# Score products of two lower halves side by side on TensorE's rows, and both stick-breaking heads chunk by chunk

## The chip, the cores and the metric

The kernel runs on one core of a Trainium2 chip. The metric is the device time of one execution in microseconds (us); the number that counts is the median of several executions of the same program. The engines are TensorE (PE; PEld is its weight load), VectorE (DVE), ScalarE (ACT), GpSimd (POOL) and SyncE (SP), which issues all DMAs here.

## The reference

One layer of a streaming encoder, for a prompt of 2048 frames and for 8 running streams of 16 new frames with 512 cached ones. The input is normed and modulated, projected to queries, keys, values and gates, and goes through two branches side by side: differential attention (A, 4 heads with two components of 64 each) and stick-breaking attention (B, 8 heads of 64). Outputs are gated, merged and projected.

```python
def diff_attention(q, k, v, qpos, kpos, lam):
    s = jnp.einsum('bqhcd,bkhcd->bhcqk', q, k) * (HEAD_DIM_A ** -0.5)
    mask = (kpos // CHUNK)[None, :] <= (qpos // CHUNK)[:, None]
    p = jax.nn.softmax(jnp.where(mask, s, -jnp.inf), axis=-1)
    w = p[:, :, 0] - lam * p[:, :, 1]
    return jnp.einsum('bhqk,bkhe->bqhe', w, v)

def stick_breaking_attention(q, k, v, qpos, kpos):
    z = jnp.einsum('bqhd,bkhd->bhqk', q, k) * (HEAD_DIM_B ** -0.5)
    mask = kpos[None, :] < qpos[:, None]
    log_1m = jnp.where(mask, jax.nn.log_sigmoid(-z), 0.0)
    log_a = jax.nn.log_sigmoid(z) + lax.cumsum(log_1m, axis=3, reverse=True) - log_1m
    a = jnp.where(mask, jnp.exp(log_a), 0.0)
    return jnp.einsum('bhqk,bkhd->bqhd', a, v)
```

## The kernel before

Everything runs in float16 pairs: a float32 number is cut into an upper half `hi` (float16 of the scaled number) and a lower half `lo` (float16 of the rest), and a product is hi·hi + hi·lo + lo·hi, added up in PSUM.

The work is cut into eight units (`units`, u = 0 to 7). Even units are of kind 0 (A: one head with its two components c), odd units of kind 1 (B: two heads, also called c). Each unit goes over 17 tiles of 128 rows: first the sample tile (t = 16, `NT`: the 16 new frames of all 8 streams), then the prompt's tiles t = 0 to 15. One pair (u, t) is a step. Per step:

- `project` multiplies the tile's hidden states (`hg`, fetched from `hT_d`) with the unit's weights (L409), and in `gate_piece` a share of the gate columns (L476). Its `finish` cuts query, key and value into halves. For a component c the key is kept as [hi; lo] (64 + 64 columns), the query as [hi; hi] and as [lo; 0], the zeros being written once.
- `transpose_qk` turns these with TensorE: two transposes for k (L489), four for q (L493), into one bank of PSUM, then copies them to `k` and `qst` in SBUF (L503, L504; ACT for A, DVE for B).
- `scores` forms, for every chunk `ch` of 512 keys up to the diagonal and for each c, one piece: the product [hi; hi]·[hi; lo] (L611), the product [lo; 0]·[hi; lo] (L612), and on the diagonal a mask, multiplied by an identity (L615). Each piece takes one PSUM bank of tag "s", of which there are three.
- `evacuate` reads the bank. For A, DVE scales it into `sc_p` or `sc_n` and takes the maximum (L530); after the diagonal chunk `softmax_pair` follows. For B, ACT writes the sigmoid of the score to `sc_p` and the sigmoid of its negative back to the bank (both L121), and `stick` runs a scan on DVE from the bank to `sc_n` (L588), from the last key to the first. When a segment of up to 8 blocks (`SEG`) is through, `stick_weights` multiplies on POOL (L594), and `turn` cuts the weights into halves (L544, L545) and transposes them by a DMA on SP's queue (L552) into `wt`.
- `pv` multiplies the weights with the values two steps later (`PV_LAG`): L659 to L661 for A, L663 and L664 for B.

The pieces of a step are laid side by side by `interleave`, which places each stream's pieces evenly by their costs; a score piece of a full chunk has cost 2.0. The projection runs ahead of the scores by a lead. In A the order of score pieces is chunk by chunk with both components; in B it is all chunks of the first head from the diagonal back, then all of the second:

```python
order = [(c, ch) for ch in range(nch) for c in range(2)] if kind == 0 else \
        [(c, ch) for c in range(2) for ch in reversed(range(nch))]
```

A scheduler orders each engine's instructions at compile time from this code, by dependences and free buffers, so the order on PE isn't always that of the code. Buffers that matter: `BANKS = {"mm": 2, "s": 3, "t": 1, "o": 2}` in PSUM, `SC_BUFS = 6` each for `sc_p` and `sc_n`, `WT_BUFS = 5`.

After the last unit comes the output stage: per tile the branches (L1227) and the output projection (L1266), and beside them, in `sample`, the sample tile's attention over cached keys. There `keys` cuts cached keys (POOL L271, DVE L274) and transposes them by DMA, `queries` spreads the sample queries into `qpad` (L705), and `scores_all` multiplies them with the new keys (L727 to L729) and the cached keys (L735, four matmuls on 32 columns of the array each).

Of the kernel before, what the change touches and what calls it, by code (L numbers as in the profile page):

```python
# [25 lines left out]
P = 128  # L26
# [4 lines left out]
NS = 16  # L31
# [80 lines left out]
def layer_kernel(ctx: ExitStack, tc: tile.TileContext, a: dict):  # L112
# [54 lines left out]
    g_d = [dram.tile([P, 2 * D], F32, name=f"g_d{t}") for t in range(NT + 1)]  # L167
    s_d = [dram.tile([P, 8, P], F16, name=f"s_d{u}") for u in range(8)]
    gate_d = dram.tile([9, D], F32, name="gate_d")
# [208 lines left out]
    qs = c01.enter_context(tc.tile_pool(name="qs", bufs=1))  # L378
    qbuf = [qs.tile([P, 2, 2, 2, 64], F16, name=f"qbuf{i}") for i in range(2)]
    for qb in qbuf:  # L380
        G.memset(qb[:, 1, :, 1, :], 0.0)
    at_hand, ahead = {}, {}
# [5 lines left out]
    def project(U, t):  # L388
# [30 lines left out]
        def finish():  # L419
# [9 lines left out]
            def halves(dst, src, scale):  # L429
                src = src.rearrange("p (c d) -> p c d", d=64)  # L430
                split(dst[:, :, 0, :], dst[:, :, 1, :], src, scale, S)

            def query(src, scale):
                src = src.rearrange("p (c d) -> p c d", d=64)
                S.activation(out=qb[:, 0, :, :, :], in_=src.unsqueeze(2).to_broadcast([P, 2, 2, 64]), func=AF.Identity, scale=scale)
                V.scalar_tensor_tensor(out=qb[:, 1, :, 0, :], in0=src, scalar=scale, in1=qb[:, 0, :, 0, :], op0=ALU.mult, op1=ALU.subtract)
            if kind == 0:
                cosT, sinT = box["r"][:, 0:32], box["r"][:, 32:96]
                x4 = pr[:, 0:256].rearrange("p (c f d) -> p c f d", c=4, f=2)
                rot = stg.tile([P, 256], F32, tag="rot", name="rot")  # L440
                r2 = stg.tile([P, 256], F32, tag="r2", name="r2", bufs=1)
                G.tensor_tensor(out=rot.rearrange("p (c f d) -> p c f d", c=4, f=2), in0=x4,  # L442
                                in1=cosT.unsqueeze(1).unsqueeze(1).to_broadcast([P, 4, 2, 32]), op=ALU.mult)
# [4 lines left out]
                halves(vt, p[:, 256:384], s2)  # L448
                query(rot[:, 0:128], s)
                halves(k16, rot[:, 128:256], s)  # L450
            else:
                rot = pr
                halves(vt, p[:, 256:384], s2)
                halves(k16, p[:, 128:256], s2)
                query(p[:, 0:128], s2)
# [6 lines left out]
            if t == NT:  # L462
                load(out=s_d[U["u"]][:, 6:8, :], in_=vt.rearrange("p c f d -> p c (f d)"))
            U["q16", t], U["k16", t] = qb, k16
# [19 lines left out]
    def transpose_qk(U, t):  # L484
        g, i = t // 4, t % 4
        q16, k16 = U.pop(("q16", t)), U.pop(("k16", t))
        pt = bank("t", F16)
        for c in range(2):
            T.transpose(pt[:, c * P : (c + 1) * P], k16[:, c, :, :].rearrange("p f d -> p (f d)"), id16)  # L489
        for f in range(2):  # L490
            for c in range(2):
                j = 2 + f * 2 + c
                T.transpose(pt[:, j * P : (j + 1) * P], q16[:, f, c, :, :].rearrange("p r d -> p (r d)"), id16)  # L493
        if t == NT:
            sam = stg.tile([P, 6, P], F16, tag="sam", name="sam", bufs=1)
            qst, kst = sam[:, 0:4, :], sam[:, 4:6, :]
        else:
            if i == 0:
                U["k"][g] = kvp.tile([P, 2, 512], F16, tag="k", name="k", bufs=K_BUFS)
            U["q", t] = qst = stg.tile([P, 4, P], F16, tag="qst", name="qst", bufs=Q_BUFS)  # L500
            kst = U["k"][g][:, :, i * P : (i + 1) * P]
        copy = V.tensor_copy if U["kind"] == 1 else S.copy
        copy(out=kst, in_=pt[:, 0:256].rearrange("p (c n) -> p c n", c=2))  # L503
        copy(out=qst, in_=pt[:, 256:768].rearrange("p (j n) -> p j n", j=4))  # L504
        if t == NT:
            load(out=s_d[U["u"]][:, 0:6, :], in_=sam)

# [89 lines left out]
    def scores(U, t, jobs):  # L597
# [5 lines left out]

        def chunk(c, ch):
            job = own[c if kind == 1 else 0]
            seg = job["segs"][ch * 4 // SEG]
# [4 lines left out]
            T.matmul(p[:, 0:n], qst[:, c, :], kk[:, c, 0:n], start=True, stop=False)  # L611
            T.matmul(p[:, 0:n], qst[:, 2 + c, :], kk[:, c, 0:n], start=False, stop=not diag)  # L612
            if diag:
                m = mask_a if kind == 0 else mask_b
                T.matmul(p[:, n - m.shape[1] : n], idb, m, start=False, stop=True)  # L615
            evacuate(job, seg, c, p, ch * 512 - seg["lo"] * P, n, sc[:, 3:4], sc[:, 4:5], ch)
            if kind == 0:
                if diag and c == 1:
                    softmax_pair(job)
                return  # L620
            i = job["segs"].index(seg)
            later = job["segs"][i + 1] if i + 1 < len(job["segs"]) else None
            stick(seg, later, ch * 512 - seg["lo"] * P, n, p)
            if ch * 4 == seg["lo"]:
                if later is not None:
                    stick_weights(job, later, None)
                if i == 0:
                    stick_weights(job, seg, later)
# [56 lines left out]
    def sample(U, dec, qpad, cs):  # L685
# [8 lines left out]
        def fetch():  # L694

            box["s"] = sam = dec.tile([P, 8, P], F16, tag="dsam", name="dsam", bufs=2)
            load(out=sam, in_=s_d[U["u"]])
# [5 lines left out]
        def queries():  # L703
            for r in range(2):
                V.tensor_copy(out=qpad.rearrange("p j (i r) n -> p j i r n", r=2)[:, :, :, r, r * NS : (r + 1) * NS],  # L705
                              in_=box["s"][:, 0:4, :].rearrange("p j (i r s) -> p j i r s", r=2, s=NS)[:, :, :, r, :])

# [4 lines left out]
        def keys(i):  # L712
            kc = box.pop((nk, i))
            k16 = dec.tile([P, 16, 2, 64], F16, tag="k16c", name="k16c", bufs=2)
            split(k16[:, :, 0, :], k16[:, :, 1, :], kc.rearrange("p j (c d) -> p (j c) d", c=2), sk, G)
            box["k", i] = kt = dec.tile([P, 8, 2, P], F16, tag="dks", name="dks", bufs=4)
            nc.sync.dma_start_transpose(out=kt.rearrange("p j c n -> p (j c) n"), in_=k16.rearrange("p j f d -> p (j f d)"))

        def scores_all():

            box["jobs"] = [new_job(U, t, c, 5, dec) for c in range(heads)]
            qsam, kn = box["s"][:, 0:4, :], box["s"][:, 4:6, :]
            mask = mask_as if kind == 0 else mask_bs
            pn = bank("s")
            for c in range(2):
                p = pn[:, c * P : (c + 1) * P]
                T.matmul(p, qsam[:, c, :], kn[:, c, 0:P], start=True, stop=False)  # L727
                T.matmul(p, qsam[:, 2 + c, :], kn[:, c, 0:P], start=False, stop=False)
                T.matmul(p, idb, mask, start=False, stop=True)  # L729
            for c in range(2):  # L730
# [7 lines left out]
                seg = job["segs"][0]  # L738
                evacuate(job, seg, c, pn[:, c * P : (c + 1) * P], 512, P, sc[:, 3:4], sc[:, 4:5], 1)
                evacuate(job, seg, c, pc, 0, 512, box["f"][:, 0:1], box["f"][:, 1:2], 0)  # L740
                if kind == 1:
                    stick(seg, None, 512, P, pn[:, c * P : (c + 1) * P])
                    stick(seg, None, 0, 512, pc)
                    stick_weights(job, seg, None)
# [26 lines left out]
        def finish():  # L771
            po = bank("s")
            vn = box["s"][:, 6:8, :].rearrange("p c (f d) -> p c f d", f=2)
            for job in box["jobs"]:
# [565 lines left out]
```

## Time and profile before

| | |
|---|---|
| median of 3 runs | 2507.16 us (2504.18 to 2513.22) |
| the profiled execution | 2508.37 us, span 2506.5 us |
| mean granted TensorE clock | 0.94 |
| instructions in the trace | 45283 |

The span runs from the first to the last instruction of the profiled execution; its own time is 1.9 us longer than its span. In the profile, L612 is line 612 of the kernel, `out<-in` are the program's tile names, and "idle before" is the time for which the engine stood still ahead of an instruction, with what released it. A matmul's duration is its passage through the array, and passages overlap. By the instructions that read the score banks, A units' scores are worked on from about 160 to 304, 581 to 775, 1019 to 1223 and 1469 to 1679 us, those of B units from about 335 to 575, 783 to 1013, 1231 to 1463 and 1691 to 1905 us, and the output stage from about 1910 us.

### The profile page before, as it was taken

The numbers are of one execution on the slowest core, as the hardware profiler recorded it, in microseconds if no ns is written. First come the engines' busy times: TensorE is split into PE (matmuls) and PEld (weight loads), VectorE is DVE, ScalarE is ACT, GpSimd is POOL, SyncE is SP. The second block draws the span as 40 slices with busy tenths as digits, with TensorE's granted clock in tenths as the row PEclk, the third lists the DMA queues.
The fourth block names the chain that finished last, engine by engine and source line by source line (L and its number), as shares of the span: only waits on it lengthen the run. The fifth ranks groups of instructions, "written<-read, shape, count | busy, mean of one in ns | idle before, by whom it ended". The sixth has DMA issues, their size and how long they took to land. (4 is left out here: it accounts for less than half of the span.)

```text
span 2506.5 us, 45283 instructions
## 1 busy us (share of the span) xinstructions
PE 2195.5 (88%) x16366; PEld 1275.3 (51%) x16366; DVE 1793.3 (72%) x3762; ACT 1602.7 (64%) x3200; POOL 827.6 (33%) x671
## 2 busy tenths in 40 slices
PE   7859898899999988889989888999975788889997
PEld 3435555455655555556655555555543344444443
DVE  3577846877676678757577876656787888888765
ACT  2558757787767688657678876656775545445542
POOL 1543113354211244311034442102344454544422
PEclk8979999999999999999999999999985799899999
DMA  9578878998787899767679976656678989888531
GB/s 287 183 221 206 211 175 200 196 220 191 180 193 185 198 222 212 172 152 183 157 192 194 219 190 177 160 132 142 153 168 206 257 224 242 242 212 229 167 111 51
DMA packets 890994, 477.07 MB, mean 190 GB/s; under 512 B 540074, under 2 KB 842330, under 8 KB 890256
## 3 DMA queue, kind: packets, MB, share of 16 engines
q1 hardware_dynamic: 890768, 474.17, 76.6%
q8 instruction: 128, 2.10, 0.4%
q14 instruction: 98, 0.80, 0.1%
HBM read 272.94 MB, written 73.44 MB: 138 GB/s over the span
## 5 line engine op out<-in xcount | busy, mean ns | idle before, releaser
L409 PE MATMUL ps_mm<-wpair,hg 128*128 128x512 f16 x3120 | 789.7, 388 | 58.1 <-DMA hg<-hT_d 54.4
L594 POOL TENSOR_TENSOR sc_p<-sc_p,sc_n 128x127 f32<-128x127 f32 (+7 forms) x192 | 314.0, 1639 | 807.3 <-DVE sc_n L588 796.0
L409 PEld LDWEIGHTS <-hg 128*128 128x128 f16 x3120 | 281.9, 100 | 328.9 <-DMA hg<-hT_d 62.5
L476 PE MATMUL ps_t<-gw,hg 128*128 128x256 f16 (+1 forms) x2856 | 397.6, 293 | 2.3 <-DVE qst L504 2.3
L476 PEld LDWEIGHTS <-hg 128*128 128x128 f16 x2856 | 280.4, 100 | 96.0 <-DVE qst L504 2.6
L588 DVE TENSOR_TENSOR_SCAN sc_n<-ps_s,sc_n,zero_t 128x512 f32<-128x512 f32 x192 | 245.6, 1279 | 63.4 <-ACT ps_s L121 58.2
L611 PE MATMUL ps_s<-k,qst 128*128 128x512 f16 (+3 forms) x640 | 226.5, 355 | 53.3 <-DVE sc_n L588 41.2
L545 DVE TENSOR_TENSOR sc_n<-sc_p,sc_n 128x128 f16<-128x128 f32 (+7 forms) x192 | 229.7, 1201 | 39.2 <-ACT sc_n L544 38.8
L121 ACT ACTIVATE sc_p<-ps_s,usc 128x512 f32<-128x512 f32 (+3 forms) x320 | 205.0, 641 | 47.1 <-PE ps_s L612 25.6
L612 PE MATMUL ps_s<-k,qst 128*128 128x512 f16 (+3 forms) x640 | 226.3, 356 | 0.0
L1227 PE MATMUL ps_mm<-wb,uT 128*128 128x512 f16 x816 | 206.8, 407 | 20.5 <-DVE o L1125 12.5
L121 ACT ACTIVATE ps_s<-ps_s,usc 128x512 f32<-128x512 f32 (+3 forms) x328 | 199.9, 610 | 0.0
L1266 PE MATMUL ps_o<-wo,yT 128*128 128x512 f16 x816 | 193.0, 390 | 6.9 <-ACT wo L269 2.4
L663 PE MATMUL ps_o<-v,wt 128*128 128x128 f16 x1088 | 156.5, 226 | 39.8 <-DMA wt<-sc_n 39.7
L544 ACT CAST sc_n<-sc_p 128x128 f16<-128x128 f32 (+7 forms) x192 | 154.8, 813 | 49.5 <-POOL sc_p L594 48.7
L442 POOL TENSOR_TENSOR rot<-pr,rope 128x256 f32<-128x256 f32 x68 | 59.8, 879 | 351.8 <-ACT pr L423 293.7
L251 ACT ACTIVATE junk<-wst 128x1024 f16<-128x1024 f32 x124 | 131.6, 1062 | 47.2 <-DMA wst<-in_w_in_dram 17.4
L663 PEld LDWEIGHTS <-wt 128*128 128x128 f16 x1088 | 104.0, 102 | 90.3 <-DMA wt<-sc_n 49.7
L1227 PEld LDWEIGHTS <-uT 128*128 128x128 f16 x816 | 82.7, 104 | 125.3 <-issue 50.8
L530 DVE TENSOR_SCALAR_CACHE_REDUCE sc_n<-ps_s,usc 128x512 f32<-128x512 f32 (+3 forms) x160 | 106.6, 666 | 55.2 <-PE ps_s L615 34.2
L664 PE MATMUL ps_o<-v,wt 128*128 128x64 f16 x1088 | 145.2, 198 | 0.0
L530 DVE TENSOR_SCALAR_CACHE_REDUCE sc_p<-ps_s,usc 128x512 f32<-128x512 f32 (+3 forms) x160 | 106.5, 666 | 52.6 <-PE ps_s L612 41.7
(295 smaller groups left out, 4372.9 us busy)
## 6 DMA issues: line engine op xcount, KB each, us to landing
hg<-hT_d SPq DMA_DIRECT2D x130, 512.0 KB, 4.5
wst<-in_w_in_dram SPq DMA_DIRECT2D x112, 256.0 KB, 3.8
g<-g_d SPq DMA_DIRECT2D x34, 512.0 KB, 5.8
wst<-in_w_in_dram SPq DMA_DIRECT2D x32, 512.0 KB, 4.8
out_dram<-pr SPq DMA_DIRECT2D x204, 64.0 KB, 2.3
g_d<-gt SPq DMA_DIRECT2D x102, 128.0 KB, 3.1
wide<-in_w_ada_dram SPq DMA_DIRECT2D x12, 1024.0 KB, 10.3
z_d<-pr SPq DMA_DIRECT2D x136, 64.0 KB, 1.8
```

The costliest lines, as they stand in the source:

```text
L121: i = S.activation(**kw)
L409: T.matmul(box["p"], box["h"][:, hi, k, :], U["w"][k][:, wi, :], start=(n == 0), stop=(n == 3 * KT - 1))
L476: T.matmul(box["g"][:, 0:gw], box["h"][:, hi, k, :], U["wg"][k // per][:, k % per, wi, :], start=(j == 0), stop=(j == 3 * KT - 1))
L530: V.tensor_scalar(out=dst[:, lo : lo + n], in0=p[:, 0:n], scalar1=sc_pos, scalar2=None, op0=ALU.mult, op1=ALU.max, accum_out=job["mx"][:, ...
L545: V.tensor_tensor(out=lo, in0=src, in1=hi, op=ALU.subtract)
L588: V.tensor_tensor_scan(out=dst[:, lo : lo + n][:, ::-1], data0=src[:, 0:n][:, ::-1], data1=zero_t[:, 0:1].to_broadcast([P, n]), initial=fi ...
L594: G.tensor_tensor(out=p[:, 0:m], in0=p[:, 0:m], in1=n[:, 1 : m + 1], op=ALU.mult)
L611: T.matmul(p[:, 0:n], qst[:, c, :], kk[:, c, 0:n], start=True, stop=False)
L612: T.matmul(p[:, 0:n], qst[:, 2 + c, :], kk[:, c, 0:n], start=False, stop=not diag)
L663: T.matmul(po[:, c * P : (c + 1) * P], wt[:, wj, :], vt[:, c, :, :], start=first, stop=False)
L1227: T.matmul(pb, st["u"][:, ui * 8 + br * 4 + k, :], wb[:, br, wi, k, c], start=(n == 0), stop=(n == 11))
L1266: T.matmul(po, st["y"][:, yi * 8 + k, :], wo[:, wi, k, c], start=(n == 0), stop=(n == 3 * KT - 1))
```

## The change

For both components together, the query is now kept as [hi; hi] of the first, [hi; hi] of the second, and one tile [lo of the first; lo of the second]. The second component's key is stored as [lo; hi], so that the upper 64 rows of the array meet lo·hi of the first component and the lower 64 rows lo·hi of the second. The new function `multiply` does a chunk for both components: two full products (with the mask behind each on the diagonal), each into a bank of its own, then two products of 64 rows, one on each half of the array's rows. One transpose per tile, the zeros in `qbuf` and one of the eight parts of `s_d` go.

A score piece is now a chunk with both components or heads, with twice the cost, and takes two "s" banks. For B this means that both heads are worked on chunk by chunk in turn, from the diagonal back, and that the scans and weights of both come behind the pair of products. In `sample`, `keys` cuts the two components in separate instructions with the halves in the order above, `queries` copies in eight small instructions for two, and `scores_all` uses one bank "s" and one bank "t" for the new keys, with 64-row products last.

```diff
-            k16 = stg.tile([P, 2, 2, 64], F16, tag="k16", name="k16")
+            k16 = stg.tile([P, 4, 64], F16, tag="k16", name="k16")
...
+            def keys(src, scale):
+                split(k16[:, 0::3, :], k16[:, 1:3, :], src.rearrange("p (c d) -> p c d", d=64), scale, S)
...
-                S.activation(out=qb[:, 0, :, :, :], in_=src.unsqueeze(2).to_broadcast([P, 2, 2, 64]), func=AF.Identity, scale=scale)
-                V.scalar_tensor_tensor(out=qb[:, 1, :, 0, :], in0=src, scalar=scale, in1=qb[:, 0, :, 0, :], op0=ALU.mult, op1=ALU.subtract)
+                S.activation(out=qb[:, 0:4, :].rearrange("p (c r) d -> p c r d", r=2), in_=src.unsqueeze(2).to_broadcast([P, 2, 2, 64]), func=AF.Identity, scale=scale)
+                V.scalar_tensor_tensor(out=qb[:, 4:6, :], in0=src, scalar=scale, in1=qb[:, 0:4:2, :], op0=ALU.mult, op1=ALU.subtract)
...
-        copy(out=qst, in_=pt[:, 256:768].rearrange("p (j n) -> p j n", j=4))
+        copy(out=qst, in_=pt[:, 256:640].rearrange("p (j n) -> p j n", j=3))
...
+    def multiply(pc, q, k, mask):
+        for c in range(2):
+            T.matmul(pc[c], q[:, c, :], k[:, c, :], start=True, stop=False)
+            if mask is not None:
+                n = pc[c].shape[1]
+                T.matmul(pc[c][:, n - mask.shape[1] : n], idb, mask, start=False, stop=False)
+        for c in range(2):
+            r = slice(c * 64, c * 64 + 64)
+            T.matmul(pc[c], q[r, 2, :], k[r, c, :], start=False, stop=True)
...
-            p = bank("s")
+            pc = [bank("s") for _ in range(2)]
...
-            T.matmul(p[:, 0:n], qst[:, c, :], kk[:, c, 0:n], start=True, stop=False)
-            T.matmul(p[:, 0:n], qst[:, 2 + c, :], kk[:, c, 0:n], start=False, stop=not diag)
...
+            multiply([p[:, 0:n] for p in pc], qst, kk[:, :, 0:n], None if not diag else mask_a if kind == 0 else mask_b)
+            for c, p in enumerate(pc):
+                job = own[c if kind == 1 else 0]
+                seg = job["segs"][ch * 4 // SEG]
+                evacuate(job, seg, c, p, ch * 512 - seg["lo"] * P, n, sc[:, 3:4], sc[:, 4:5], ch)
...
+            for c, p in enumerate(pc):
...
+                stick(seg, later, ch * 512 - seg["lo"] * P, n, p)
...
-        order = [(c, ch) for ch in range(nch) for c in range(2)] if kind == 0 else \
-                [(c, ch) for c in range(2) for ch in reversed(range(nch))]
-        return [(2.0 if ch < t // 4 else (t % 4 + 1) / 2, lambda c=c, ch=ch: chunk(c, ch)) for c, ch in order]
+        return [(4.0 if ch < t // 4 else t % 4 + 1, lambda ch=ch: chunk(ch)) for ch in (range(nch) if kind == 0 else reversed(range(nch)))]
...
+            def copy(dst, src, rows):
+                for r in range(2):
+                    V.tensor_copy(out=qpad[rows, dst, :, :].rearrange("p (i r) n -> p i r n", r=2)[:, :, r, r * NS : (r + 1) * NS],
+                                  in_=box["s"][rows, src, :].rearrange("p (i r s) -> p i r s", r=2, s=NS)[:, :, r, :])
+            for c in range(2):
+                copy(c, c, slice(0, P))
+                copy(2 + c, 2, slice(c * 64, c * 64 + 64))
...
-            k16 = dec.tile([P, 16, 2, 64], F16, tag="k16c", name="k16c", bufs=2)
-            split(k16[:, :, 0, :], k16[:, :, 1, :], kc.rearrange("p j (c d) -> p (j c) d", c=2), sk, G)
+            k16 = dec.tile([P, 8, 2, 2, 64], F16, tag="k16c", name="k16c", bufs=2)
+            for c in range(2):
+                split(k16[:, :, c, c, :], k16[:, :, c, 1 - c, :], kc[:, :, c * 64 : c * 64 + 64], sk, G)
...
-            pn = bank("s")
+            pn = [bank(tag)[:, 0:P] for tag in "st"]
```

More of the change, by code (lines that the diff above doesn't have):

```diff
@@ L167, in layer_kernel @@
     g_d = [dram.tile([P, 2 * D], F32, name=f"g_d{t}") for t in range(NT + 1)]
-    s_d = [dram.tile([P, 8, P], F16, name=f"s_d{u}") for u in range(8)]
+    s_d = [dram.tile([P, 7, P], F16, name=f"s_d{u}") for u in range(8)]
     gate_d = dram.tile([9, D], F32, name="gate_d")
@@ L378, in layer_kernel @@
     qs = c01.enter_context(tc.tile_pool(name="qs", bufs=1))
-    qbuf = [qs.tile([P, 2, 2, 2, 64], F16, name=f"qbuf{i}") for i in range(2)]
-    for qb in qbuf:
-        G.memset(qb[:, 1, :, 1, :], 0.0)
+    qbuf = [qs.tile([P, 6, 64], F16, name=f"qbuf{i}") for i in range(2)]
     at_hand, ahead = {}, {}
@@ L447, in finish @@
                 G.tensor_tensor(out=rot, in0=rot, in1=r2, op=ALU.add)
-                halves(vt, p[:, 256:384], s2)
+                values(p[:, 256:384], s2)
                 query(rot[:, 0:128], s)
-                halves(k16, rot[:, 128:256], s)
+                keys(rot[:, 128:256], s)
             else:
                 rot = pr
-                halves(vt, p[:, 256:384], s2)
-                halves(k16, p[:, 128:256], s2)
+                values(p[:, 256:384], s2)
+                keys(p[:, 128:256], s2)
                 query(p[:, 0:128], s2)
@@ L462, in finish @@
             if t == NT:
-                load(out=s_d[U["u"]][:, 6:8, :], in_=vt.rearrange("p c f d -> p c (f d)"))
+                load(out=s_d[U["u"]][:, 5:7, :], in_=vt.rearrange("p c f d -> p c (f d)"))
             U["q16", t], U["k16", t] = qb, k16
@@ L487, in transpose_qk @@
         pt = bank("t", F16)
[L488 to L493, printed above, removed]
+        for x16, n, lo in ((k16, 2, 0), (q16, 3, 2)):
+            for c in range(n):
+                T.transpose(pt[:, (lo + c) * P : (lo + c + 1) * P], x16[:, 2 * c : 2 * c + 2, :].rearrange("p f d -> p (f d)"), id16)
         if t == NT:
-            sam = stg.tile([P, 6, P], F16, tag="sam", name="sam", bufs=1)
-            qst, kst = sam[:, 0:4, :], sam[:, 4:6, :]
+            sam = stg.tile([P, 5, P], F16, tag="sam", name="sam", bufs=1)
+            qst, kst = sam[:, 0:3, :], sam[:, 3:5, :]
         else:
@@ L499, in transpose_qk @@
                 U["k"][g] = kvp.tile([P, 2, 512], F16, tag="k", name="k", bufs=K_BUFS)
[L500 removed]
+            U["q", t] = qst = stg.tile([P, 3, P], F16, tag="qst", name="qst", bufs=Q_BUFS)
             kst = U["k"][g][:, :, i * P : (i + 1) * P]
@@ L602, in scores, with chunk @@
         jobs += own
-        def chunk(c, ch):
-            job = own[c if kind == 1 else 0]
-            seg = job["segs"][ch * 4 // SEG]
+        def chunk(ch):
             n = 512 if ch < t // 4 else (t % 4 + 1) * P
-            p = bank("s")
+            pc = [bank("s") for _ in range(2)]
             qst, kk = U["q", t], U["k"][ch]
             diag = ch == t // 4
[L611 to L616, printed above, removed]
+            multiply([p[:, 0:n] for p in pc], qst, kk[:, :, 0:n], None if not diag else mask_a if kind == 0 else mask_b)
[3 more added lines that the diff above has]
+                evacuate(job, seg, c, p, ch * 512 - seg["lo"] * P, n, sc[:, 3:4], sc[:, 4:5], ch)
@@ L617, in chunk @@
             if kind == 0:
-                if diag and c == 1:
+                if diag:
                     softmax_pair(job)
                 return
[L621 to L628, printed above, removed]
@@ L630, in scores @@
-        order = [(c, ch) for ch in range(nch) for c in range(2)] if kind == 0 else \
-                [(c, ch) for c in range(2) for ch in reversed(range(nch))]
-        return [(2.0 if ch < t // 4 else (t % 4 + 1) / 2, lambda c=c, ch=ch: chunk(c, ch)) for c, ch in order]
+            for c, p in enumerate(pc):
+                job = own[c]
+                seg = job["segs"][ch * 4 // SEG]
+                i = job["segs"].index(seg)
+                later = job["segs"][i + 1] if i + 1 < len(job["segs"]) else None
+                stick(seg, later, ch * 512 - seg["lo"] * P, n, p)
+                if ch * 4 == seg["lo"]:
+                    if later is not None:
+                        stick_weights(job, later, None)
+                    if i == 0:
+                        stick_weights(job, seg, later)
@@ L694, in fetch @@
         def fetch():
-            box["s"] = sam = dec.tile([P, 8, P], F16, tag="dsam", name="dsam", bufs=2)
+            box["s"] = sam = dec.tile([P, 7, P], F16, tag="dsam", name="dsam", bufs=2)
             load(out=sam, in_=s_d[U["u"]])
```

27 lines of the change are left out of this document (11 added, 16 removed).

## The prediction

> **What bounds the kernel now.** I read the page first: busy shares and costliest groups. The chain that ended last (second row) covers 4% of the span, at its end, so it says nothing about the scores. For those I used busy time by stretch, then PE's waits.
>
> ```profile
> PE 2195.5 (88%) x16366; PEld 1275.3 (51%) x16366; DVE 1793.3 (72%) x3762; ACT 1602.7 (64%) x3200; POOL 827.6 (33%) x671
> ...
> PE 2%; DVE 1%; DMA 1%; ACT 0%; issue 0%; POOL 0%; DVEq 0%; POOLq 0%; ACTq 0%
> ```
>
> ```profile
> core 0: us, PE busy (x) PEld busy (x) DVE busy (x) ACT busy (x) POOL busy (x), PEclk, DMA share, GB/s
> ...
> 1010.00:1240.00 230.00, 215.64 (x1670) 138.25 (x1669) 151.85 (x393) 149.88 (x336) 41.12 (x46) 0.97 0.69 167
> 1240.00:1450.00 210.00, 184.83 (x1441) 115.29 (x1439) 160.86 (x247) 158.94 (x317) 82.74 (x59) 0.94 0.89 197
> ...
> 1690.00:1910.00 220.00, 192.64 (x1367) 104.50 (x1365) 173.03 (x257) 154.37 (x294) 85.96 (x53) 0.92 0.69 154
> 1910.00:2506.00 596.00, 500.80 (x3740) 253.16 (x3740) 458.74 (x973) 279.04 (x450) 250.66 (x179) 0.90 0.73 197
> ```
>
> The first stretch is an A unit (PE 94% busy), the next two are B units (88%, with DVE and ACT at 70 to 79%), the last is the stage of cached keys and outputs. PE sets the pace of A. In B, PE still has the most work, but it is held up:
>
> ```profile
> engine line waited for: us in total, times, longest us
> PE ps_mm L409 <- DMA hg<-hT_d: 54.4, 29, 5.7
> PE ps_s L611 <- DVE sc_n L588: 41.2, 39, 3.1
> PE ps_o L663 <- DMA wt<-sc_n: 39.7, 32, 6.5
> PE ps_o L659 <- DMA wt<-sc_n: 22.4, 19, 3.7
> ...
> PE ps_s L611 <- DVE sc_n L530: 3.4, 4, 1.5
> ```
>
> The second row is a score matmul waiting for a bank of PSUM: there are three "s" banks, and a B bank comes back when the scan (L588) has read it. For A (L530 reads the bank) the same wait is 3.4 us. So removed PE time counts nearly in full in A, and a new wait on banks would appear first in B.
>
> **The score matmuls: what is removed.** One score piece now is two full matmuls, L611 and L612. Their forms:
>
> ```profile
> L612 PE MATMUL ps_s<-k,qst 128*128 128x512 f16 x448 | 174.4, 389 | 0.0
> ...
> L612 PE MATMUL ps_s<-k,qst 128*128 128x384 f16 x64 | 21.4, 335 | 0.0
> ...
> L612 PE MATMUL ps_s<-k,qst 128*128 128x256 f16 x64 | 17.7, 277 | 0.0
> ...
> L612 PE MATMUL ps_s<-k,qst 128*128 128x128 f16 x64 | 14.1, 222 | 0.0
> ```
>
> The 389 ns are a matmul's passage, not its price; the price is the distance between starts.
>
> ```profile
> start us, us, engine line op out<-in xcount [idle before <-releaser]
> 82.54 0.59 PE L409 MATMUL ps_mm<-wpair,hp 128*128 128x512 f16 x2
> 83.06 0.41 PE L923 MATMUL ps_t<-ident,tmp 9*128 9x9 f32 x4
> ...
> 1563.01 0.39 PE L493 MATMUL ps_t<-id,qbuf 128*128 128x128 f16 x4
> ...
> 2192.66 0.59 PE L1266 MATMUL ps_o<-wo,yT 128*128 128x512 f16 x2
> 2193.19 1.91 PE L735 MATMUL ps_s<-dks,qpad 128*32 128x512 f16 x32
> 2195.03 0.39 PE L1227 MATMUL ps_mm<-wb,uT 128*128 128x512 f16 x1
> ```
>
> Two matmuls of 512 columns take 0.59 us, one 0.38, so starts lie 0.21 to 0.22 us apart; I use 0.216. Four of 128 columns take 0.39 and one 0.22: 0.056 apart. The price follows the columns: 0.162 for 384, 0.108 for 256.
>
> A row's count is of both components, so there are 224 pairs of 512 columns and 32 of each shorter form, 320 in all. Of four full matmuls per pair the change leaves two, plus two half-height ones. If the halves run together, a pair loses one matmul: 224 x 0.216 + 32 x (0.162 + 0.108 + 0.056) = 48.4 + 10.4 = 58.8 us.
>
> Do they run together? No 64-row pair is in this trace. The nearest row is L735, where four matmuls use 32 columns of the array each: 32 of 512 columns in 1.91 us, where one after the other they would need 32 x 0.216 = 6.9. Separate strips of the array therefore do overlap, almost perfectly. Bounds for the pair: one matmul (full overlap) to two (none, 58.8 us lost again). I take full overlap, as L735 shows for strips the other way round.
>
> **What is added: changing the shape of the array.** The second L1266 starts at 2192.66 + 0.59 - 0.38 = 2192.87, and L735, of another shape, at 2193.19: about 0.31 us later, not 0.216. On the way out the last group of L735 starts at 2193.19 + 1.91 - 0.39 = 2194.71 and L1227 at 2195.03: again about 0.31. The 9-row transposes L923 show it for rows: the second L409 starts at 82.75, L923 at 83.06. So each change costs about 0.095 us more than a matmul of the same shape. That is about the 100 ns of one weight load, which between matmuls of one shape lies under the matmul before:
>
> ```profile
> L612 PEld LDWEIGHTS <-qst 128*128 128x128 f16 x640 | 63.1, 99 | 87.8 <-issue 56.1
> ```
>
> Every pair goes in and out: 320 x 2 x 0.095 = 60.8 us. Against 58.8 us saved this is +2 us: pairs of 512 columns gain 0.026 us, those of 384, 256 and 128 lose 0.03, 0.08 and 0.13. Bounds: nothing, if the two halves count as no other shape, to a full emptying of the array, 0.38 - 0.216 + 0.10 = 0.26 us a change, 166 us in all. The three rows agree on 0.095 and I take that.
> The Trainium skill, page "TensorEngine Tiling (Array Packing)", section "Key Properties", says that changing the tiling mode drains TensorE. Read as a full drain it gives the 166 us just named and 105 us more in the sum; the rows here show less, since L735 begins before the last L1266 has ended.
>
> **Transposes and their copies.** Six transposes a tile become five: 136 tiles x 0.056 = -7.6 us on PE (L493 counts 544, four a tile). The copy of q's transposes shrinks from 512 to 384 elements:
>
> ```profile
> L504 ACT COPY qst<-ps_t 128x512 f16<-128x512 f16 x64 | 38.0, 593 | 0.0
> ...
> L504 DVE COPY qst<-ps_t 128x512 f16<-128x512 f16 x64 | 26.5, 414 | 0.0
> ...
> L503 ACT COPY k<-ps_t 128x256 f16<-128x256 f16 x64 | 23.4, 365 | 11.7 <-PE ps_t L493 11.5
> ```
>
> By the 593 and 365 ns of 512 and 256 elements ACT saves some 0.11 us in each of 68 tiles, 7.8 us, and DVE rather less. Both engines have 20% and more idle time, so I count nothing. Splitting q and k keeps its sizes.
>
> **Two banks at a time.** This is where I expect the loss. Up to now a piece takes one of three banks, and the bank is wanted again three pieces later. A B unit has 80 pieces in its 210 to 230 us, 2.75 us each, so a bank has 8.2 us. After the change a pair takes two banks together: the second product of the next pair needs the first bank of this pair, two piece-times, or 5.5 us, later. How long a bank is held:
>
> ```profile
> 1835.03 0.38 PE L611 MATMUL ps_s<-k,qst 128*128 128x512 f16 x1
> ...
> 1836.33 0.68 ACT L121 ACTIVATE sc_p<-ps_s,usc 128x512 f32<-128x512 f32 x1
> ...
> 1836.91 0.65 ACT L121 ACTIVATE ps_s<-ps_s,usc 128x512 f32<-128x512 f32 x1
> ...
> 1837.66 1.27 DVE L588 TENSOR_TENSOR_SCAN sc_n<-ps_s,sc_n,zero_t 128x512 f32<-128x512 f32 x1
> ```
>
> From 1835.03 to 1838.93, 3.9 us. In a pair, ACT can start on the first head only when the lower halves are through, 0.216 + 0.31 + 0.39 = 0.92 us after the first product; two sigmoids (1.33) and a scan (1.27) return that bank after 3.5 us with no queue, and the second, behind the first on ACT, after 4.9. With queues as in the rows, a us more each. The margin falls from 8.2 - 3.9 = 4.3 us to 5.5 - 4.5 = 1 us, and pieces are not evenly spaced. PE works in order: behind the waiting product stand that pair's lower halves, the next projection and the weighted values, and ACT and DVE wait for these in turn.
>
> Bounds for what is added: nothing, if the order of PE's work is laid so that other matmuls fill the gap, up to each of the 160 B pairs waiting the 1.06 us of a present wait (41.2 / 39), 170 us. Nearest is the present wait itself: I let it double, +41 us. Some of that covers time that PE would have waited for hg or wt anyway (116.5 us in three rows), so I count 60%, +25 us. A is left out: two reads of 0.75 us each by L530 return its banks, and it hardly waits today.
>
> Both heads' weights now come together at the end of a tile, and the "n" buffers of both (six in all, four of them for a tile above 8 blocks) are held at once. The values use them two tiles later, so this delays transposing DMAs on SP's queue, behind which hg loads stand, but should not end the tile; zero, with the risk in the upper end.
>
> **The last stage.** Cached keys are cut in two instructions in place of one on POOL and on DVE:
>
> ```profile
> L271 POOL TENSOR_SCALAR k16c<-dc,s_c 128x1024 f16<-128x1024 f32 x32 | 41.7, 1302 | 78.5 <-DMA dc<-in_cache_a_k_dram 27.3 <-DMA dc<-in_cache_b_k_dram 23.5 <-issue 13.6
> ...
> L271 POOL TENSOR_SCALAR wpair<-wst,sw 128x512 f16<-128x512 f32 x28 | 23.8, 857 | 69.7 <-DMA wst<-in_w_in_dram 47.4 <-PE ps_mm L409 9.6 <-PE ps_s L615 8.4
> ...
> L705 DVE COPY qpad<-dsam x16: 195/220/1211, 1938.2 to 2304.7; 128x256 f16<-128x256 f16 x16
> ```
>
> POOL: 64 x 0.857 - 41.7 = +13 us, under cover, as POOL is 42% busy there. DVE has 77% in that stage and gains small copies: 64 for 16 at 0.2 us each at most, +10 us. The new scores of a unit change shape four times, 8 x 4 x 0.095 = 3 us on PE. I take +5 us for the stage, between 0 and 15.
>
> **Sum**, against the profiled execution (2508.4 us, span 2506.5; 1.2 us above the median): +2 - 7.6 + 25 + 5 = +24, so 2532 us, and 2531 on the median.
>
> **The rivals.** First, on the other side: changing to half rows costs nothing, because weights of one half are loaded under the matmul before. Then the 58.8 and 7.6 us come off: with the bank waits and the last stage as above 2507 - 66 + 30 = 2471, without them 2441. Against it stand L923 and L735, where the change shows every time; for it, that neither is a 64-row half. It decides if the change costs under 0.05 us.
> Second, the waits on banks do not grow, because the order of PE's work, which is not the code's (transposes stand between parts of a score in places), fills them: 2507 + 2 - 8 + 0 to 5, 2500 to 2507, no change or slightly faster. For it: A pieces already come in pairs in today's order.
> Third, the change does not do what it says: the halves run one after the other, or PE's order puts other work between them. That returns 58.8 us, 2531 + 59 = 2590.
>
> **How the numbers follow.** The forecast has 0.55, full gain 0.12, no growth of waits 0.2, no overlap 0.13. About 0.3% (7.5 us, 2499.6 to 2514.7) is what a measurement of this kernel can tell from no change. Faster: 0.12 and nearly half of the second rival, 0.21. Same: the rest of it and the lowest part of the forecast, 0.13. Slower: 0.66. The range leaves out the full gain below and the extremes above: 2485 to 2595. The forecast's own range is 2512 to 2570, waits of 5 to 65 us.
>
> **What would show it.** Right: two half-height matmuls starting within some ns, the next full one 0.31 us later; PE's busy time nearly as before; the wait of the first or second score product for the scan well above 41 us, most in B, and B stretches longer, A stretches equal. Wrong: a pair in under 0.7 us from first product to next matmul (change is free), waits below 50 us, or A longer by several us a unit (halves apart).

## The result and the profile after

The changed kernel takes 2574.31 us (median of 4 runs, 2560.43 to 2577.67) against 2508.27 us: 1.0263 times as long, 95% interval 1.0237 to 1.0288, or 66 us more. The forecast was 24 us more. The profiled execution took 2570.96 us, its span is 2568.9 us; its lines:

```profile
PE 2268.6 (88%) x16230; PEld 1230.2 (48%) x16230; DVE 1790.3 (70%) x3842; ACT 1600.4 (62%) x3200; POOL 835.0 (33%) x701
...
L509 PE MATMUL ps_s<-k,qst 128*128 128x512 f16 (+3 forms) x640 | 212.9, 356 | 43.8 <-DVE sc_n L597 31.3
...
L515 PE MATMUL ps_s<-k,qst 64*128 64x512 f16 (+3 forms) x640 | 192.1, 363 | 0.0
```

PE has 136 matmuls fewer (the transposes) and is busy 73 us longer (2268.6 against 2195.5). L509 is the full product, L515 the half-height one. In time order on PE (start, length, line):

```profile
932.42 0.38 PE L509 MATMUL ps_s<-k,qst 128*128 128x512 f16 x1
932.73 0.39 PE L515 MATMUL ps_s<-k,qst 64*128 64x512 f16 x1
933.05 2.76 PE L407 MATMUL ps_mm<-wpair,hg 128*128 128x512 f16 x12
935.65 0.22 PE L670 MATMUL ps_o<-v,wt 128*128 128x128 f16 x1
935.71 0.19 PE L671 MATMUL ps_o<-v,wt 128*128 128x64 f16 x1
935.74 0.38 PE L509 MATMUL ps_s<-k,qst 128*128 128x512 f16 x1
936.05 0.39 PE L515 MATMUL ps_s<-k,qst 64*128 64x512 f16 x1
936.37 0.23 PE L670 MATMUL ps_o<-v,wt 128*128 128x128 f16 x1
```

One half-height product follows its own full product; the partner comes 3.3 us later. Into the half shape it is 0.31 us from start to start, out of it 0.32, as on other lines before. By the start times of the 640 records of L515, only 116 pairs start within 5 ns of each other (3 ns in the median); 204 pairs stand apart, so the array goes into the half shape 524 times, not 320. The order fixed at compile time does that (the run with held pairs, below, shows it): the first half is ready as soon as its own full product is issued, and the second bank comes later. Over the 160 B pairs the second full product starts 2.4 us behind the first in the mean; two pieces one behind the other stood 2.5 us apart before.

PE's waits; the fourth row, of the last stage, has no counterpart before:

```profile
PE ps_mm L407 <- DMA hg<-hT_d: 51.3, 32, 6.1
PE ps_o L670 <- DMA wt<-sc_n: 31.5, 19, 7.5
PE ps_s L509 <- DVE sc_n L597: 31.3, 26, 5.7
PE ps_t L739 <- DVE o L791: 14.6, 5, 6.8
...
PE ps_o L666 <- DMA wt<-sc_n: 11.2, 11, 2.3
```

The wait for banks, which the forecast let double, fell from 41.2 to 31.3 us. The fourth row is new: `scores_all` (L739) wants the one "t" bank, in which the last transpose of the unit before (L790) still waits to be added on DVE (L791).

Two stretches, from about the end of the last score matmul to the end of the span, before and after:

```profile
1901.00:2506.50 605.50, 504.27 (x3772) 255.62 (x3770) 466.68 (x980) 285.10 (x458) 256.32 (x182) 0.89 0.73 196
```

```profile
1937.00:2568.90 631.90, 511.42 (x3772) 256.32 (x3771) 482.20 (x1058) 285.10 (x458) 275.87 (x212) 0.88 0.68 186
```

The last counts in brackets are of PE, PEld, DVE, ACT and POOL instructions. 36 us are lost up to there and 26 in the last stage, which has the same 3772 matmuls and 9% more DVE and POOL instructions. Measured from the first score product of one unit to that of the next, the four A units are 27 us longer than before (852 against 825) and the four B units 6 us (929 against 923); units overlap, so this tells only roughly where the time went. The forecast named the reverse, B longer and A equal, as the sign of bank waits, and a longer A as the sign of halves that stand apart.

### The profile page after: what moved, and what is told of

Read it like the earlier page. It is cut to its first block, busy times and chain, and to the rows that moved or that the text cites. A ratio compares the mean times of both kernels' runs of the same rounds, so it can differ in the third digit from the quotient of the medians.

```text
span 2568.9 us, 45056 instructions
## 1 busy us (share of the span) xinstructions
PE 2268.6 (88%) x16230; PEld 1230.2 (48%) x16230; DVE 1790.3 (70%) x3842; ACT 1600.4 (62%) x3200; POOL 835.0 (33%) x701
## 5 line engine op out<-in xcount | busy, mean ns | idle before, releaser
L407 PE MATMUL ps_mm<-wpair,hg 128*128 128x512 f16 x3120 | 779.1, 387 | 54.4 <-DMA hg<-hT_d 51.3
L603 POOL TENSOR_TENSOR sc_p<-sc_p,sc_n 128x127 f32<-128x127 f32 (+7 forms) x192 | 305.1, 1596 | 821.2 <-DVE sc_n L597 789.5
L407 PEld LDWEIGHTS <-hg 128*128 128x128 f16 x3120 | 274.1, 99 | 345.5 <-DMA hg<-hT_d 63.6
L476 PE MATMUL ps_t<-gw,hg 128*128 128x256 f16 (+1 forms) x2856 | 388.2, 290 | 2.6 <-DVE qst L501 2.3
L476 PEld LDWEIGHTS <-hg 128*128 128x128 f16 x2856 | 273.0, 98 | 96.2 <-issue 10.5
L509 PE MATMUL ps_s<-k,qst 128*128 128x512 f16 (+3 forms) x640 | 212.9, 356 | 43.8 <-DVE sc_n L597 31.3
L554 DVE TENSOR_TENSOR sc_n<-sc_p,sc_n 128x128 f16<-128x128 f32 (+7 forms) x192 | 215.5, 1129 | 47.4 <-ACT sc_n L553 46.6
L515 PE MATMUL ps_s<-k,qst 64*128 64x512 f16 (+3 forms) x640 | 192.1, 363 | 0.0
L597 DVE TENSOR_TENSOR_SCAN sc_n<-ps_s,zero_t 128x128 f32<-128x128 f32 (+3 forms) x128 | 103.5, 817 | 52.0 <-ACT ps_s L121 48.5
```

The costliest lines, as they stand in the source:

```text
L407: T.matmul(box["p"], box["h"][:, hi, k, :], U["w"][k][:, wi, :], start=(n == 0), stop=(n == 3 * KT - 1))
L476: T.matmul(box["g"][:, 0:gw], box["h"][:, hi, k, :], U["wg"][k // per][:, k % per, wi, :], start=(j == 0), stop=(j == 3 * KT - 1))
L509: T.matmul(pc[c], q[:, c, :], k[:, c, :], start=True, stop=False)
L515: T.matmul(pc[c], q[r, 2, :], k[r, c, :], start=False, stop=True)
L554: V.tensor_tensor(out=lo, in0=src, in1=hi, op=ALU.subtract)
L597: V.tensor_tensor_scan(out=dst[:, lo : lo + n][:, ::-1], data0=src[:, 0:n][:, ::-1], data1=zero_t[:, 0:1].to_broadcast([P, n]), initial=fi ...
```

## The experiments

Ratios are to the kernel before, run beside each (its medians were 2509 to 2513 us). Each diff is against the kernel that its paragraph names.

**Held pairs.** Of the changed kernel:

```diff
+        with tc.high_priority():
             for c in range(2):
...
+                half = T.matmul(pc[c], q[r, 2, :], k[r, c, :], start=False, stop=True)
+                if c == 0:
+                    tc.add_manual_dep(half.ins, last.ins.name, NOSYNC, reason="halves together")
```

> The changed kernel, with the two 64-row products of a chunk held together: they are given a high priority and the first is issued only behind the last full product of its pair (an order, not a wait). In the changed kernel's profile only 116 of 320 pairs stand side by side, and the array changes its shape 524 times each way. Theory 1 (the order at compile time takes the pairs apart): 204 pairs get back one stream each (some 37 us of PE) and 204 changes of shape and back go (204 x 0.19 = 39 us); PE busy falls from 2269 to about 2193 us, the scores end some 30 us earlier, total about 2540 us. Theory 2 (the loss is in banks taken two at a time): the pairs now wait for both banks before either may be read, PE's wait for the scan rises from 31 us to 60 us or more and the total stays at 2565 to 2590 us.

Measured: all 320 pairs start within 5 ns, PE busy falls by 71 us as expected, and the time does not move: 2574.15 us, 1.0261 (1.0225 to 1.0297).

```profile
PE 2197.3 (85%) x16230; PEld 1223.9 (48%) x16230; DVE 1779.7 (69%) x3842; ACT 1600.0 (62%) x3200; POOL 821.0 (32%) x701
```

```profile
PE ps_mm L407 <- DMA hg<-hT_d: 75.9, 41, 6.3
PE ps_o L673 <- DMA wt<-sc_n: 47.2, 29, 7.8
PE ps_s L509 <- DVE sc_n L600: 38.4, 36, 6.8
...
PE ps_s L509 <- DVE sc_p L542: 18.2, 17, 3.8
PE ps_o L669 <- DMA wt<-sc_n: 16.2, 13, 2.3
```

PE's time turned into its waits: for hg +25 us, for wt +21, for banks (both readers, the scan and A's L542) some 22, against the changed kernel. The order on PE shows what holding a pair does:

```profile
934.97 0.38 PE L509 MATMUL ps_s<-k,qst 128*128 128x512 f16 x1
...
938.21 0.38 PE L509 MATMUL ps_s<-k,qst 128*128 128x512 f16 x1
938.52 0.39 PE L516 MATMUL ps_s<-k,qst 64*128 64x512 f16 x2
```

The first full product starts 3.2 us before the second, and only then do both halves run, in one passage. Taken apart, the first half follows at once. Over the 160 B pairs of the two traces, ACT starts to read the first bank 4.8 us after the start of its full product in the mean with held pairs, and 2.5 us after it in the changed kernel. One more thing differs: the granted clock is 0.932 in this profile (0.929 to 0.932 in the four runs) and 0.939 in the changed kernel's. No run separates its part from that of the waits.

**The order alone.** Of the kernel before, with its layout and 128-row products, but both components or heads of a chunk in one piece: `multiply` as in the changed kernel, with

```diff
-            T.matmul(pc[c], q[r, 2, :], k[r, c, :], start=False, stop=True)
+            T.matmul(pc[c], q[:, 2 + c, :], k[:, c, :], start=False, stop=True)
```

> The kernel before with nothing but the new order: a chunk's piece is both components or heads, takes two banks, does two full products and then the two lower ones, all over 128 rows; layouts, transposes and the last stage stay as before. Theory 1 (shape changes and pairs taken apart cost the time): within 10 us of before, 2500 to 2518 us. Theory 2 (two banks at a time and both heads in turn cost it): 2530 to 2550 us, with more wait of the score product for the scan in B.

Measured: 2523.67 us, 1.0050 (1.0032 to 1.0068). Neither range holds it: 12 to 15 us, and not as a wait for banks.

```profile
PE ps_mm L409 <- DMA hg<-hT_d: 62.0, 34, 5.3
PE ps_o L670 <- DMA wt<-sc_n: 55.8, 41, 6.8
PE ps_s L510 <- DVE sc_n L597: 33.3, 27, 4.7
PE ps_o L666 <- DMA wt<-sc_n: 18.2, 15, 3.1
```

Banks are waited for less (33.3 for 41.2 us), weights (wt, both rows) 12 us more and hg 8 us more. The layout alone, the last run below, moves these rows as far with no loss at all, so they do not show the cause by themselves.

**B's order alone.** Of the kernel before, one bank per piece as there:

```diff
-                [(c, ch) for c in range(2) for ch in reversed(range(nch))]
+                [(c, ch) for ch in reversed(range(nch)) for c in range(2)]
```

> The kernel before with nothing but the order of B's pieces: chunk by chunk, both heads in turn, each piece as before with one bank and its own two products. If both heads in turn cost (buffers of both heads held, weights of both at the tile's end): 2515 to 2530 us, like the order with two banks at a time (2524). If two banks at a time were what cost there: 2505 to 2515 us, no change.

Measured: 2518.36 us, 1.0034 (1.0019 to 1.0049). Taking both heads in turn costs about 8 us by itself; two banks at a time add no more than the intervals leave.

```profile
PE ps_mm L409 <- DMA hg<-hT_d: 49.9, 30, 5.3
PE ps_o L663 <- DMA wt<-sc_n: 40.1, 27, 6.9
PE ps_s L611 <- DVE sc_n L588: 38.2, 36, 4.6
PE ps_o L659 <- DMA wt<-sc_n: 25.1, 15, 3.4
```

None of these rows is more than 3 us longer than before, and hg is shorter. The profiled execution, at 2513.22 us, is one of the fastest of the ten, so the rows may show less than the 8 us.

**A change of shape alone.** Of the kernel before:

```diff
-            T.matmul(p[:, 0:n], qst[:, 2 + c, :], kk[:, c, 0:n], start=False, stop=not diag)
+            T.matmul(p[:, 0:n], qst[0:64, 2 + c, :], kk[0:64, c, 0:n], start=False, stop=not diag)
```

> The kernel before with nothing but the lower product (L612) over its 64 rows that are not zero; it has no partner on the other half, so nothing overlaps and each of the 640 changes the array's shape and back. If a change costs 0.095 us, PE busy rises by 640 x 0.19 = 122 us to about 2317 us, and the total by 60 to 120 us, to 2570 to 2630 us. If half rows are no other shape, nothing changes: 2500 to 2515 us.

Measured: 2565.07 us, 1.0227 (1.0192 to 1.0262), below the range expected for a change that costs.

```profile
PE 2306.9 (90%) x16366; PEld 1241.9 (49%) x16366; DVE 1799.6 (70%) x3762; ACT 1609.8 (63%) x3200; POOL 831.1 (32%) x671
```

```profile
PE ps_mm L409 <- DMA hg<-hT_d: 39.4, 25, 4.1
PE ps_o L663 <- DMA wt<-sc_n: 31.2, 22, 7.7
PE ps_s L611 <- DVE sc_n L588: 24.0, 20, 3.0
...
PE ps_o L659 <- DMA wt<-sc_n: 11.4, 7, 3.2
```

PE busy rises by 111 us: 0.174 us in and out, 0.087 a change, near the 0.095 read from the trace before. Half of it reaches the end; the other half took the place of waits, for these four rows are 52 us shorter than before.

**The last stage, all of it, the bank, the keys.** Three runs of the changed kernel. The bank edit is

```diff
-            pn = [bank(tag)[:, 0:P] for tag in "st"]
+            pn = [bank(tag)[:, 0:P] for tag in "ss"]
```

and the keys edit

```diff
-            for c in range(2):
-                split(k16[:, :, c, c, :], k16[:, :, c, 1 - c, :], kc[:, :, c * 64 : c * 64 + 64], sk, G)
+            split(k16[:, :, 0, :], k16[:, :, 1, :], kc.rearrange("p j (c d) -> p (j c) d", c=2), sk, G)
```

The first run has both and the two query copies of before.

> The changed kernel with its last stage brought back near to the one before: cached keys cut in one instruction on POOL and one on DVE, sample queries copied in two instructions, the scores of the new keys in two banks of tag s and none of tag t. The second component's scores against cached keys are not the right ones in it. Theory 3 (half of the loss, 29 of 62 us, arises after the last scores): the stage from the first branch product to the end shrinks by 20 to 30 us, total 2545 to 2555 us. If the last stage was only longer by chance or by its start, nothing changes: 2565 to 2580 us.

> The changed kernel with the new keys' scores of the last stage in two s banks, none of tag t. If the wait for the one t bank (14.6 us in the changed kernel's list, behind L791) is what lengthens the last stage: 10 to 15 us off, 2558 to 2565 us, and the wait gone without another in its place. If it only moves to the s banks: 2568 to 2578 us.

> The changed kernel with cached keys cut in one instruction each on POOL and DVE; the second component's cached scores lack the product of the query's lower half in it. If the doubled instructions lengthen the last stage: 10 to 20 us off, 2552 to 2565 us. If POOL and DVE have room for them: 2568 to 2578 us.

Measured: all three 2560.16 us, 1.0194 (1.0156 to 1.0231); the bank 2552.20, 1.0154 (1.0128 to 1.0179); the keys 2567.21, 1.0221 (1.0195 to 1.0246). The bank gave more than expected and all three together less: the bank alone gives at least what all three give, and keys and copies give little or nothing that shows. With the bank edit the stretch from the last score matmul has the length of before, at as many DVE and POOL instructions as in the changed kernel, and the wait for L791 is gone from PE's list. That row was 14.6 us, and the edit takes off 22 us by the medians, 27 by the ratios; where the rest sat was not traced (PE busy in the stretch is also 10 us less, at a granted clock of 0.89 for 0.88):

```profile
1941.00:2544.10 603.10, 501.64 (x3771) 255.05 (x3770) 480.25 (x1058) 284.86 (x458) 274.75 (x212) 0.89 0.72 195
```

**No change of shape in the prompt's scores, all else as changed.** The bank edit, and

```diff
-            T.matmul(pc[c], q[r, 2, :], k[r, c, :], start=False, stop=True)
+            T.matmul(pc[c], q[:, 2, :], k[:, c, :], start=False, stop=True)
```

> The changed kernel with the lower products over all 128 rows (the other half then adds a product of two lower halves, some 2 to the minus 22 of the score) and the last stage's new keys in two s banks: its layout, its five transposes, its order and its two banks at a time, and no change of shape in the prompt's scores. If shape changes are most of the 40 us left: PE busy falls from 2258 to about 2190 us, total 2515 to 2525 us, where the order alone was (2524). If the order is most of it: 2535 to 2552 us.

Measured: 2527.17 us, 1.0065 (1.0043 to 1.0086), PE busy 2182.8 us (2257.5 with the bank edit alone). This is the cleanest pair of runs: they differ in the height of the lower products alone, and by 0.9%, some 22 us. The wait for the scan is 46.3 us here, 5 more than before. Between first score products as above, the half rows add 35 us of PE work and 15 us of time to the A units, and 42 us of work and 7 us of time to the B units; in B most of the added work only takes the place of waits.

**Held pairs in A alone.** On the kernel before, with B and the last stage untouched; on the changed kernel; and there with the bank edit. Then held pairs in A and B with the bank edit. The hold is the one above, put on A's pairs alone in the first three; in the first, A's pieces are made by a function `both` that works as the changed kernel's `chunk`:

```diff
+        if kind == 0:
+            return [(4.0 if ch < t // 4 else t % 4 + 1, lambda ch=ch: both(ch)) for ch in range(nch)]
```

> The kernel before with the change in A's prompt tiles alone, its pairs held together; B, the sample tile and the last stage as before. From the starts of the units' score matmuls, A units took 824 us in all before and 806 with pairs held together, B units 924 against 982. If A gains by itself (it waits little for banks): 15 to 20 us off, 2485 to 2500 us. If two banks at a time cost in A too, as A's wait for L530 of 18 us with held pairs (3 us in the changed kernel's list at most) suggests: 2505 to 2520 us.

> The changed kernel with pairs held together in A alone, B in the order that it has in the changed kernel. If held pairs gain in A (852 to 806 us over the four units) and cost only in B: about 46 us off, 2520 to 2535 us. If the B loss of the held pairs is only A's gain moved on: 2560 to 2575 us.

> The changed kernel with pairs held together in A alone and the last stage's new keys in two s banks. If both gains add up (14 us and 22 us): about 2538 us; what is then left against the kernel before is B's part: shape changes of pairs taken apart and the new order. If the gains overlap: 2548 to 2555 us.

> The changed kernel with pairs held together in A and B, and the last stage's new keys in two s banks, none of tag t. The base for the next one. The t bank gave 22 us in the run with that edit alone; held pairs gave nothing on the whole: 2550 to 2558 us.

Measured, in that order: 2506.68 us, 0.9982 (0.9962 to 1.0002); 2560.39, 1.0185 (1.0162 to 1.0208); 2549.81, 1.0143 (1.0125 to 1.0162); 2561.00, 1.0194 (1.0177 to 1.0211). In A alone on the kernel before, the change is no loss and no gain that is clear. Held A pairs take 14 us by the medians, some 20 by the ratios, off the changed kernel (1.0263 to 1.0185), far less than the 46 of the first expectation. My reading of unit lengths (46 us from A) was wrong: units overlap, and a unit's length is no measure of what it costs. The gains of bank and held A pairs do not add up (1.0143 against 1.0154 for the bank alone). With the bank edit and A's pairs held, holding B's pairs too costs 13 us more (1.0194 against 1.0143), though PE is busy 51 us less (2200.6 against 2252.0); the granted clocks of the two profiles, 0.932 and 0.933, are alike.

**A fourth bank.** Held pairs in A and B and the bank edit, then the kernel before as a control:

```diff
-    BANKS = {"mm": 2, "s": 3, "t": 1, "o": 2}
+    BANKS = {"mm": 2, "s": 4, "t": 1, "o": 1}
```

> As the run before it, with four s banks in place of three and one o bank in place of two. Theory 2 (with held pairs the loss sits in B, where two banks are taken at a time): PE's wait for the scan and for L542 falls from some 55 us to under 20, B units shrink by 30 to 50 us in all, total 2505 to 2530 us, if the kernel before is not slowed by the missing o bank. If banks are not it: no change, 2545 to 2560 us, or more for the o bank.

> The kernel before with four s banks and one o bank: the control. If the second o bank is not needed: 2495 to 2515 us, with the score product's wait for the scan down from 41 us. If values of two tiles need both: 2520 us or more.

Measured: 2560.78 us, 1.0184 (1.0161 to 1.0206), and 2556.54, 1.0186 (1.0160 to 1.0213). Inconclusive: the edit, which takes one "o" bank away, costs the kernel before some 44 us, and the held pairs lose nothing by it. A fourth "s" bank may be worth as much to them, but no run shows it by itself.

**The layout alone.** Of the kernel before, for the prompt's tiles, pieces and order and last stage as before, the new layout of q and k with the lower products over 128 rows:

```diff
-            T.matmul(p[:, 0:n], qst[:, 2 + c, :], kk[:, c, 0:n], start=False, stop=not diag)
+            T.matmul(p[:, 0:n], qst[:, 2, :], kk[:, c, 0:n], start=False, stop=not diag)
```

> The kernel before, its pieces, order and last stage, with the new layout for the prompt's tiles: three q tiles to transpose and copy in place of four, the lower products of both components from the one tile [lo; lo] over 128 rows (the other half adds a product of two lower halves). PE loses 128 x 0.056 = 7 us, ACT 7 us and DVE 4 us of copies. If that counts as PE time does in A: 3 to 10 us off, 2500 to 2508 us. If it is hidden: 2508 to 2513 us.

Measured: 2506.01 us, 0.9985 (0.9974 to 0.9995). The one version whose interval lies below the kernel before, by about 4 us: one transpose and a quarter of a copy less per tile, and no half shape at all. PE busy is 2185.8 us.

```profile
PE ps_o L681 <- DMA wt<-sc_n: 50.0, 31, 4.4
PE ps_s L629 <- DVE sc_n L606: 47.9, 39, 3.5
PE ps_mm L410 <- DMA hg<-hT_d: 40.6, 27, 5.2
PE ps_o L677 <- DMA wt<-sc_n: 25.8, 15, 6.4
```

Without any loss of time, the wait for wt is 14 us longer than before, that for banks 7 us longer and that for hg 14 us shorter. So a shift of some 10 us between these rows is no measure of a cost.

## Why the prediction was right or wrong

The direction was right, and the size was not: 66 us for 24. The direction was in good part luck, since the +25 us of bank waits, which alone made the forecast slower, is not what the runs show. Laid up from the runs, each time in all: both heads in turn 8 us (1.0034), with two banks at a time, the layout and the other edits of the last stage 16 us (1.0065), with the half-height products 39 us (1.0154), with the t bank 66 us (1.0263).

- **The price of a change of shape** was right: 0.095 us read, 0.087 measured. A full emptying at each change, 0.26 us by the forecast's bound, would have been 640 x 0.52 = 333 us in the run with half rows alone; PE busy rose by 111. The Trainium skill, page "TensorEngine Tiling (Array Packing)", section "Key Properties", says that changing the tiling mode drains TensorE. Read as a full drain, this run does not bear it out.
- **Halves run together** when side by side: right, 3 ns apart. With all pairs held, PE busy was 2197.3 us, within 8 us of what the terms +2 and -7.6 give from the 2195.5 of before.
- **That they stand side by side** failed. The term "+2 us" of the score matmuls took 320 changes each way and full overlap; there were 524 and 116 pairs. Each of the 204 pairs that stand apart loses the overlap, 0.184 us in the mean, and makes one more change in and out, 0.19 us by the forecast's price: an estimate of 76 us. The third rival named halves that stand apart, but priced the lost overlap alone, 59 us for all pairs. With half rows PE busy is 75 us higher than with full ones (2257.5 against 2182.8) and the time 22 us, since much of the added work took the place of waits.
- **Banks at +25 us**: the mechanism failed, the size was nearer by luck. The wait, which was to double from 41.2 us, was 31.3 us in the changed kernel, 33.3 in the run with the order alone and 46.3 with full rows. The failed step is that a pair takes its two banks together: the order on PE kept the second full product 2.4 us behind the first and laid other matmuls between, as the second rival said. What the order costs, 8 to 16 us, was not traced to a cause. In the run of the order wt is 12 and hg 8 us longer, but B's order alone lengthens neither clearly, and the layout alone shifts both as far at no loss. That both heads' weights reach SP's queue together, which the forecast set at zero, is a guess that no run tested. Banks do matter where pairs are held, some 22 us more of wait, and there the first bank is read 2.3 us later.
- **The last stage at +5 us** failed worst for its size: 27 us, from 1.0154 to 1.0263, for the "t" bank alone. The forecast counted instructions of POOL and DVE, which had room, and passed over the line that takes the single "t" bank; L791's wait there is in no row of before, but the use of the bank by the step next to it in the same file was to be read in the code.
- **Transposes** at -7.6 us: about 4 us in the time (1 to 7 by the interval of the layout alone).

The first rival (a free change of shape) is refuted by the run with half rows, the second (waits do not grow, hence no change) held for the banks alone: their wait did not grow, and the loss came elsewhere.

## What to carry to other kernels

Splitting the array pays only if what it saves is large against two changes of shape: here 0.17 us against one matmul of 0.216 us, with both halves side by side. If a compiler orders the work, check that the parts to be run side by side are side by side in its order, and then what holding them costs those who wait for the first of them. When an edit takes a buffer from another pool, list everything that uses that pool in the steps beside it: a wait on a single bank cost more than all the added instructions.

## What the runs showed of the hardware that was not expected

Cutting cached keys in two pieces of 512 elements took DVE 1093 ns each where one of 1024 took 1719 in the mean: 69.1 us for 55.0 in all, and still nothing in the time that can be told from noise (1.0221 with one piece, 1.0263 with two, and the intervals overlap). Before and after:

```profile
L274 DVE SCALAR_TENSOR_TENSOR k16c<-dc,s_c,k16c 128x1024 f16<-128x1024 f32 x32 | 55.0, 1719 | 20.0 <-POOL k16c L271 18.5 <-DMA gsm<-gate_d 1.5
```

```profile
L274 DVE SCALAR_TENSOR_TENSOR k16c<-dc,s_c,k16c 128x512 f16<-128x512 f32 x64 | 69.1, 1093 | 31.2 <-POOL k16c L271 31.1
```
